# A decoder layer on one core: the opening put in the planner's order, and the conditioning of the output gates moved behind the attention

## The chip, the core and the metric

The kernel runs on one core of a Trainium2 chip. The number that counts is the device time of one execution in microseconds (us). The core has five engines with a queue each: TensorE (PE, matrix products into PSUM), VectorE (DVE), ScalarE (ACT), GpSimd (POOL) and SyncE (SP), which here issues nearly all DMAs. An engine takes its instructions strictly in the order of its queue, and one that has to wait holds everything behind it.

## The reference, cut to what matters

One layer of a decoder with a conditioning vector: 512 tokens of 1024 channels, fp32.

```python
cond = jax.nn.silu(c)                                        # 1024 numbers
ada = (cond @ ada_w[l] + ada_b[l])[:, None, :]               # 1024 x 6144
sh1, sc1, gt1, sh2, sc2, gt2 = jnp.split(ada, 6, axis=-1)    # 1024 each
h = modulate(rmsnorm(x, norm1_w[l]), sh1, sc1)               # h * (1 + sc1) + sh1
p = h @ w_in[l]                                              # all mixers' projections
...                                                          # A: HGRN2, B: sparse attention, C: RWKV7
merged = ga * (y_a @ w_branch[l, 0]) + gb * (y_b @ w_branch[l, 1]) + gc * (y_c @ w_branch[l, 2])
x = x + gt1 * (merged @ w_out[l])
h = modulate(rmsnorm(x, norm2_w[l]), sh2, sc2)
x = x + gt2 * ((jax.nn.silu(h @ ffn_w1[l]) * (h @ ffn_w3[l])) @ ffn_w2[l])
return rmsnorm(x, final_norm_w)
```

The product `cond @ ada_w` has 6144 columns, counted here in 12 blocks of 512: blocks 0 to 3 are sh1 and sc1, 4 and 5 gt1 (the gate on the output projection), 6 to 9 sh2 and sc2, 10 and 11 gt2 (the gate on the FFN).

## The kernel before, in words

**Products.** Every fp32 product is three fp32r products: a matrix is split into `hi` (a cast, on ACT for weights: `whi`, for activations: `hhi`) and `lo` (the difference, on DVE: `wlo`, `hlo`), and TensorE adds hi·hi, lo·hi and hi·lo in PSUM. A weight tile goes from a DMA (`wraw`, three buffers) over `whi` and `wlo` (two each) to `mm` (L438). `tr` (L442) and the transposes at L495 and L667 run on TensorE too. PSUM has four rings of two buffers, g, f, m and n. All other instructions are recorded at one helper line, L191, so they are told apart by their tiles.

**Stages, by the trace's time.** 0 to 66: the opening. Then phase A to about 510, in which the projections of the mixers A and C and of the attention are interleaved with these two mixers. The attention (`b_mixer`) with `merge(0)` and `merge(2)` to 693, `merge(1)` and the output projection to about 800, the FFN to the end.

**The opening.** `run` issues all its loads on SP: c, then the conditioning weights `aw` of the chunks k = 0 and 1 (128 rows of h each), the four x tiles, the identity, the small vectors `vrows` (norm weights, `ada_b` and the like, two tiles of rows that `turn_vecs` transposes into columns `vT`), then for each k the first input weights `fw` (768 columns) and `aw` of the next k. `FIRST` says for which k a conditioning load exists and how many chunks it covers: every k by itself. `norm_x` makes the RMS norm of x (a Square with accumulation on ACT, a power on POOL, then half the tile on DVE and half on ACT). `first_gemm` walks over k: `ada(k)` multiplies `aw` by `cond` and adds up on DVE (`ada_sum`, eight instructions into `facc`), adds over the partitions with products against `ones` on TensorE (`ada_cols`), which gives scale and shift; `modulate` transposes the chunk of x (4 transposes) and applies them (`nh` on ACT, then `hhi` and `hlo`); `products` makes the 18 products of this k into six PSUM tiles. Instructions are placed here by the framework's scheduler. `c_setup` then turns the six tiles into the first operands of mixer C.

**Phase A** is planned by `Order` with a `Clock`, which counts what each instruction costs and picks at each step among jobs (weight tiles, which feed TensorE) and chains (generators of mixer steps). It begins by `order.clock.reset()` after the opening. One of the chains, "D", is `ada_steps`: for each of the blocks 6, 7, 8, 9, 4, 5, 10, 11 it loads eight tiles `adaw` of 128x512 (two buffers, so that a load has to wait for the sum that read its buffer), adds them up on DVE into `adacc`, and adds over the partitions on TensorE. The gates' rows (4, 5, 10, 11) are written to a row `adarow` in DRAM, from which `gate_row` broadcasts them later.

**After phase A** the framework's scheduler places all instructions again. `merge(b)` multiplies each of the eight output tiles of branch b by its gate: for `merge(1)` each m needs a gate tile (24 products, from a `wraw` of `in_w_in`) and a branch tile (12 products, `in_w_branch`), and DVE does `msg` and the `wlo` of both.

## Time and profile before

| | |
|---|---|
| three timed runs | 1170.91, 1172.86, 1173.13 us, median 1172.86 |
| the profiled execution | 1168.5 us, span 1166.7, granted clock 0.993 |
| TensorE busy | 1113.3 us (95% of the span) |
| VectorE busy | 656.0 us (56%) |
| ScalarE busy | 415.4 us (36%) |
| DMA | 125.28 MB, mean 107 GB/s |

The span runs from the first to the last instruction; the execution's own time is 1.8 us longer. Busy matmuls overlap each other, so TensorE's pace is read from the starts of its instructions and its losses from its idle time.

### The profile page before, as it was taken

To read this page: it belongs to the slowest core of one execution; us is meant where nothing else is said; L and a number is where in the kernel's file an instruction comes from. 1 tells how busy PE (TensorE), PEld (TensorE's weight loads), DVE (VectorE), ACT (ScalarE), POOL (GpSimd) and SP (SyncE) were. 2 spreads that over 40 slices of the span, in tenths; PEclk is the share of its full clock that TensorE was granted. 3 is DMA by queue.
4 is the path that set the end of the run, shared out by engine and by line. 5 is a ranking of instruction groups with operands and counts; after the bars stand their busy time and mean duration, and the time that the engine had idled before them with its cause. 6 is when DMAs were issued, how large, how long until landed. Compare 5 with 4: busy or idle time off the path is not lost.

```text
span 1166.7 us, 18717 instructions
## 1 busy us (share of the span) xinstructions
PE 1113.3 (95%) x7545; PEld 908.2 (78%) x7545; DVE 656.0 (56%) x1404; ACT 415.4 (36%) x753; POOL 82.7 (7%) x96
## 2 busy tenths in 40 slices
PE   3989999999999999899999989999999999999997
PEld 3759887878887897577878667878888888888886
DVE  5858666675756766377576745445333433432533
ACT  4342431242331231165454654435222323222221
POOL 1001010120111000110112002110000000000000
PEclk9989999999999999999999999999999999999999
DMA  9934433324253234653223105542333333333331
GB/s 280 264 103 134 140 89 85 84 68 134 52 124 84 71 101 118 197 164 100 73 63 82 28 1 146 160 137 72 92 94 105 90 97 102 90 100 99 91 108 72
DMA packets 183087, 125.28 MB, mean 107 GB/s; under 512 B 27929, under 2 KB 163111, under 8 KB 183000
## 3 DMA queue, kind: packets, MB, share of 16 engines
q1 hardware_dynamic: 182424, 123.04, 37.2%
q8 instruction: 59, 0.97, 0.4%
q10 hardware_dynamic: 576, 1.05, 0.2%
q14 instruction: 28, 0.23, 0.1%
HBM read 121.15 MB, written 5.53 MB: 109 GB/s over the span
## 4 chain that ended last, share of the span: by engine, by line
PE 83%; DMA 5%; DVE 5%; SPq 2%; ACT 2%; issue 2%; POOL 0%; POOLq 0%; DVEq 0%; ACTq 0%
PE g L438 26%; PE f L438 25%; PE m L438 18%; PE n L438 11%; SPq L191 2%; PE n L442 2%; DMA adaw<-in_ada_w_dram 1%; DVE wlo L191 1%; DMA wraw<-in_w_in_dram 1%; DMA msg<-adarow 1%; PE m L442 1%; DMA x<-in_x_dram 1%; DMA fw<-in_w_in_dram 1%; ACT bpt L191 0%; DMA wraw<-in_w_out_dram 0%
## 5 line engine op out<-in xcount | busy, mean ns | idle before, releaser
L191 DVE TENSOR_TENSOR wlo<-wraw,whi 128x1024 fp32r<-128x1024 f32 (+2 forms) x144 | 164.2, 1140 | 154.9 <-ACT whi L191 153.0
L191 ACT CAST whi<-wraw 128x1024 fp32r<-128x1024 f32 (+2 forms) x144 | 139.1, 967 | 279.0 <-PE f L438 119.6
L438 PE MATMUL g<-hhi,whi 128*128 128x512 f32 (+1 forms) x368 | 154.7, 420 | 9.9 <-ACT whi L191 9.9
L438 PE MATMUL g<-hhi,wlo 128*128 128x512 f32 (+1 forms) x368 | 143.9, 391 | 2.5 <-DVE wlo L191 2.3
L438 PE MATMUL g<-hlo,whi 128*128 128x512 f32 (+1 forms) x368 | 143.3, 390 | 0.0
L438 PEld LDWEIGHTS g<-hhi,whi 128*128 128x128 f32 x368 | 70.1, 190 | 29.4 <-ACT whi L191 11.3
L438 PE MATMUL f<-hhi,whi 128*128 128x512 f32 (+1 forms) x240 | 92.7, 386 | 0.0
L438 PE MATMUL f<-hhi,wlo 128*128 128x512 f32 (+1 forms) x240 | 92.4, 385 | 0.0
L438 PE MATMUL f<-hlo,whi 128*128 128x512 f32 (+1 forms) x240 | 92.0, 383 | 0.0
L438 PEld LDWEIGHTS g<-hhi,wlo 128*128 128x128 f32 x368 | 69.7, 189 | 19.7 <-DVE wlo L191 4.9
L438 PEld LDWEIGHTS g<-hlo,whi 128*128 128x128 f32 x368 | 70.0, 190 | 11.2 <-issue 0.5
L191 DVE SCALAR_TENSOR_TENSOR adacc<-adaw,cond,adacc 128x512 f32<-128x512 f32 x56 | 42.6, 761 | 17.6 <-DMA adaw<-in_ada_w_dram 17.0
L438 PEld LDWEIGHTS f<-hhi,whi 128*128 128x128 f32 x240 | 45.4, 189 | 8.5
L438 PEld LDWEIGHTS f<-hhi,wlo 128*128 128x128 f32 x240 | 45.2, 188 | 8.6
L438 PEld LDWEIGHTS f<-hlo,whi 128*128 128x128 f32 x240 | 45.1, 188 | 8.2
L438 PE MATMUL f<-whi,hhi 128*128 128x256 f32 (+1 forms) x144 | 44.4, 308 | 0.0
L191 DVE CUSTOM_DVE_ANT_0 bs<-m,bW 128x128 f32<-128x128 f32 (+3 forms) x64 | 30.1, 486 | 24.5 <-PE m L438 15.3
L438 PE MATMUL f<-wlo,hhi 128*128 128x256 f32 (+1 forms) x144 | 41.6, 289 | 0.0
L438 PE MATMUL f<-whi,hlo 128*128 128x256 f32 (+1 forms) x144 | 41.5, 288 | 0.0
L191 ACT ACTIVATE bs<-bs,bst 128x128 f32<-128x128 f32 (+3 forms) x64 | 35.9, 563 | 12.8 <-DVE bst L191 12.4
L438 PE MATMUL f<-yhi,whi 128*128 128x512 f32 x96 | 38.3, 399 | 2.2 <-ACT yhi L191 1.4
L191 POOL TENSOR_TENSOR merged<-merged,msg 128x512 f32<-128x512 f32 x16 | 26.0, 1622 | 202.3 <-DVE msg L191 194.5
(439 smaller groups left out, 2375.9 us busy)
## 6 DMA issues: line engine op xcount, KB each, us to landing
wraw<-in_ffn_w_dram SPq DMA_DIRECT2D x66, 512.0 KB
wraw<-in_w_in_dram SPq DMA_DIRECT2D x52, 512.0 KB
adaw<-in_ada_w_dram SPq DMA_DIRECT2D x64, 256.0 KB
aw<-in_ada_w_dram SPq DMA_DIRECT2D x16, 512.0 KB
wraw<-in_w_branch_dram SPq DMA_DIRECT2D x16, 256.0 KB
wraw<-in_w_out_dram SPq DMA_DIRECT2D x8, 512.0 KB
fw<-in_w_in_dram SPq DMA_DIRECT2D x24, 128.0 KB
toep<-toep SPq DMA_DIRECT2D x8, 320.0 KB
```

Of the source, the lines that this page charges most:

```text
L191: r = f(*a, **kw)
L438: return self.nc.tensor.matmul(o, l, r, **kw)
L442: return self.nc.tensor.transpose(o, x, ident)
```

## The change

1. **Opening in the planner.** `norm_x`, `first_gemm`, `setup_vecs` and `c_setup` go; the opening is a set of chains and jobs of `Order`, written in the planned order, and phase A follows without a reset. x is loaded first. The vectors `vrows` are issued from POOL (12 DMAs, ahead of POOL's powers for the norm) instead of SP. Norms are whole-tile operations, two of the four sums of squares go to DVE (`tensor_tensor_reduce`). All 32 transposes of x are made ahead of the products, ACT copies them to SBUF (`xT`), and `first_mod` applies scale and shift from there. The first weight tile of mixer A (q, head 0) is split into buffers of its own during the opening.
2. **Conditioning of sh1 and sc1.** `FIRST = {0: 1, 1: 1, 2: 2, 4: 2, 6: 1, 7: 1}`: for k = 0 and 1 TensorE multiplies `aw` by `cond` directly, 16 products with one column each (`n<-cond,aw`), in place of DVE's sums; k = 2, 3 and k = 4, 5 are summed in pairs, 128x512 at a time. `aw` has three buffers of the double size in place of six, so the loads for k = 4, 6 and 7 wait for the sums or products of k = 0, 1 and 2.
3. **Gates.** Chain D does blocks 6 to 9 alone. Blocks 4 and 5 are issued in `merge(2)`, 10 and 11 in the FFN's tiles j = 4 and 9, each from a pool that is open there; the framework's scheduler places them.
4. **Planner.** Costs of DMAs, the rule when a job's tile is loaded or split, and `pace` (8 for 4) change; the bias of the attention gets a tile of its own.

The diff, cut (`Clock` and `Order` show the lines that set rates and pace):

```diff
-FIRST = {k: 1 for k in range(KT)}
+FIRST = {0: 1, 1: 1, 2: 2, 4: 2, 6: 1, 7: 1}
...
-            self.bus = max(self.bus, t + 1.3) + size / 3.3e5
-            return self.end(outs, ins, self.bus + 0.7)
+            took = size / (4.0e5 if run >= 4096 else 3.4e5 if run > 512 else 3.0e5)
...
-    def run(self, until=None, pace=4):
-        while until not in self.done and (self.chains or self.tiles or self.steps):
+    def run(self, until=lambda: False, pace=8):
+        while not until() and (self.chains or self.tiles or self.steps):
...
-            nc.sync.dma_start(rows[r0:r0 + n], ap)
+            nc.gpsimd.dma_start(rows[r0:r0 + n], ap)
...
-    def ada_steps(self):
-
-        nc, pool = self.nc, self.pc
-        self.ada_row = self.t(self.dr, [12, 512], "adarow")
-        blocks = (6, 7, 8, 9, 4, 5, 10, 11)
+    def ada_steps(self, pool, *blocks, acc="adacc"):
+
+        nc = self.nc
...
+    def first_ada(self, pool, ks):
...
+            if k < 2:
+
+                ps = None
+                for q in range(2):
+                    for a in range(2):
+                        yield self.cond, aw[:, a, 4 * q:4 * q + 4], ("now", "turned")[k], ":n" if ps is None else "now"
+                        if ps is None:
+                            ps = self.psn()
+                        for kk in range(4 * q, 4 * q + 4):
+                            self.mm(ps[:, a:a + 1], aw[:, a, kk], self.cond[:, kk:kk + 1], start=(kk + a == 0), stop=(kk + a == KT))
...
+            acc = self.t(pool, [P, 2, 2, P], "facc", bufs=2)[:, :, :n]
+            for kk in range(KT):
+                yield self.cond, aw[:, 0, kk], aw[:, 1, kk], "dve+"
+                self.ada_sum(acc, kk, aw[:, :, kk])
...
-            order.chain("D", self.ada_steps(), 5, None)
...
+            order.chain("D", self.ada_steps(self.pc, 6, 7, 8, 9), 5, None)
...
+            ada = self.ada_steps(wo, 4, 5, acc="wtmp")
             for _ in self.merge(2, yc, h):
+                for _ in range(5):
+                    next(ada, None)
+            for _ in ada:
                 pass
...
+                if j in (4, 9):
+                    for _ in self.ada_steps(p3, 10 + (j == 9)):
+                        pass
```

TensorE's queue from its first instruction on, before (`n` is a PSUM ring; `x` the four token tiles, `facc` the sums of the conditioning):

```order
L495 MATMUL n_201<-ident_97,vrows_9_99 128x56
L438 MATMUL n_212<-ones_175,facc_214 128x1 x2
L667 MATMUL n_213<-ident_97,x_89 128x128
L667 MATMUL n_213<-ident_97,x_91 128x128
L667 MATMUL n_213<-ident_97,x_93 128x128
L438 MATMUL n_212<-ones_175,facc_227 128x1 x2
L667 MATMUL n_213<-ident_97,x_95 128x128
L667 MATMUL n_213<-ident_97,x_89 128x128
L667 MATMUL n_213<-ident_97,x_91 128x128
L667 MATMUL n_213<-ident_97,x_93 128x128
L667 MATMUL n_213<-ident_97,x_95 128x128
L438 MATMUL m_206<-hhi_177,whi_269 128x512
```

And in the changed kernel, the same place:

```order
L452 MATMUL n_181<-ident_83,vrows_14_99 128x56
L448 MATMUL n_187<-cond_84,aw_126 128x1 x12
L452 MATMUL m_204<-ident_83,x_113 128x128
L452 MATMUL m_204<-ident_83,x_115 128x128
L452 MATMUL m_204<-ident_83,x_117 128x128
L452 MATMUL m_204<-ident_83,x_119 128x128
L452 MATMUL f_210<-ident_83,x_113 128x128
L452 MATMUL f_210<-ident_83,x_115 128x128
L452 MATMUL f_210<-ident_83,x_117 128x128
```

The transposes of one k stood before each k's products; now the conditioning products and the transposes of several k stand ahead of the first product (behind the rows shown come the rest of the eight groups of four transposes and four more products with `aw`, and then the first product of k = 0).

VectorE's queue at the end of the attention and the beginning of `merge(1)`, before (`ylo` is the last operation on the attention's output, `msg` the gating of an output tile, `wlo` a weight's split, `bkc` a part of `merged`):

```order
L191 TENSOR_SCALAR bs_6630<-bs_6630,bst_6631 128x512
L191 SCALAR_TENSOR_TENSOR ylo_7123<-y_5261,yhi_7122 128x4x128
L191 SCALAR_TENSOR_TENSOR msg_7132<-msg_7132,f_7205 128x512
L191 TENSOR_TENSOR wlo_7255<-wraw_7253,whi_7254 128x512
L191 TENSOR_TENSOR wlo_7280<-wraw_7277,whi_7279 128x1024
L191 SCALAR_TENSOR_TENSOR bkc_7607<-merged_4436,bq_7604 128x512
```

And in the changed kernel:

```order
L197 SCALAR_TENSOR_TENSOR ylo_7083<-y_5159,yhi_7082 128x4x128
L197 TENSOR_SCALAR wtmp_6663<-adaw_6659,cond_84 128x512
L197 SCALAR_TENSOR_TENSOR wtmp_6663<-adaw_6661,cond_84,wtmp_6663 128x512
L197 SCALAR_TENSOR_TENSOR wtmp_6663<-adaw_6665,cond_84,wtmp_6663 128x512
L197 SCALAR_TENSOR_TENSOR wtmp_6663<-adaw_6668,cond_84,wtmp_6663 128x512
L197 SCALAR_TENSOR_TENSOR wtmp_6663<-adaw_6725,cond_84,wtmp_6663 128x512
L197 SCALAR_TENSOR_TENSOR wtmp_6663<-adaw_6728,cond_84,wtmp_6663 128x512
L197 SCALAR_TENSOR_TENSOR msg_7092<-msg_7092,f_7165 128x512
L197 TENSOR_TENSOR wlo_7215<-wraw_7213,whi_7214 128x512
L197 SCALAR_TENSOR_TENSOR wtmp_6663<-adaw_6785,cond_84,wtmp_6663 128x512
L197 TENSOR_TENSOR wlo_7240<-wraw_7237,whi_7239 128x1024
L197 SCALAR_TENSOR_TENSOR wtmp_6663<-adaw_6788,cond_84,wtmp_6663 128x512
```

Six sums of block 4 (`wtmp`) now stand between `ylo` and the first `msg`, and two more before `bkc`; those of block 5 follow among the next tiles.

SyncE's queue at this place in the changed kernel (`adaw` are the tiles of block 4, `wraw` weight tiles: of a branch, of `w_out` and of a gate):

```order
L197 DMA wraw_7268<-in_w_branch_dram 64x4x128 x2
L197 DMA adaw_6659<-in_ada_w_dram 128x512
L197 DMA adaw_6661<-in_ada_w_dram 128x512
L197 DMA adaw_6665<-in_ada_w_dram 128x512
L197 DMA adaw_6668<-in_ada_w_dram 128x512
L197 DMA adaw_6725<-in_ada_w_dram 128x512
L197 DMA adaw_6728<-in_ada_w_dram 128x512
L197 DMA adaw_6785<-in_ada_w_dram 128x512
L197 DMA adaw_6788<-in_ada_w_dram 128x512
L197 DMA wraw_7290<-in_w_out_dram 128x1024
L197 DMA adaw_6791<-in_ada_w_dram 128x512
L197 DMA wraw_7296<-in_w_in_dram 128x8x128
```

Before, the loads of the branch tile, of `w_out` and of the gate followed each other here; now nine `adaw` loads stand among them, and from the third on each waits for the sum that read its buffer.

## Rows read from the trace of the kernel before

**Rows 1.** One execution by engine: busy us, share of the span, instructions

```profile
PE 1113.3 (95%) x7545; PEld 908.2 (78%) x7545; DVE 656.0 (56%) x1404; ACT 415.4 (36%) x753; POOL 82.7 (7%) x96
```

**Rows 2.** Page's costliest groups, chain D's sums: busy, mean ns | idle before

```profile
L191 DVE SCALAR_TENSOR_TENSOR adacc<-adaw,cond,adacc 128x512 f32<-128x512 f32 x56 | 42.6, 761 | 17.6 <-DMA adaw<-in_ada_w_dram 17.0
```

**Rows 3.** Windows: length; busy (instructions) of PE, PEld, DVE, ACT, POOL; PEclk; DMA; GB/s

```profile
0.00:20.00 20.00, 2.61 (x12) 2.45 (x12) 9.62 (x28) 8.65 (x15) 2.97 (x11) 1.00 0.91 268
72.00:76.00 4.00, 3.96 (x9) 2.22 (x8) 2.97 (x4) 0.47 (x1) 0.00 (x0) 0.50 0.50 143
460.00:480.00 20.00, 16.43 (x184) 10.80 (x184) 8.05 (x18) 2.86 (x4) 1.65 (x1) 1.00 0.53 147
480.00:500.00 20.00, 17.48 (x87) 11.46 (x86) 9.30 (x14) 4.88 (x7) 2.81 (x6) 1.00 0.78 235
```

**Rows 4.** Opening in order of time: start, length, engine, operation [idle before <-releaser]

```profile
12.71 1.06 ACT L191 ACTIVATE hhi<-x 128x1024 fp32r<-128x1024 f32 x1 [9.48 <-DMA x<-in_x_dram]
...
17.37 1.01 PE L438 MATMUL n<-ones,facc 128*128 128x1 f32 x4
...
20.40 0.82 ACT L191 CAST whi<-fw 128x768 fp32r<-128x768 f32 x1
20.42 0.96 DVE L191 TENSOR_TENSOR wlo<-fw,whi 128x768 fp32r<-128x768 f32 x1
21.12 0.77 ACT L191 ACTIVATE nh<-n,adaT,s 128x512 f32<-128x512 f32 x1
...
21.93 0.62 ACT L191 CAST hhi<-nh 128x512 fp32r<-128x512 f32 x1
...
21.95 1.12 PE L667 MATMUL n<-ident,x 128*128 128x128 f32 x4 [1.34 <-ACT nh L191]
...
22.72 1.20 PE L438 MATMUL m<-hhi,whi 128*128 128x512 f32 x2
```

**Rows 5.** TensorE after the opening, in order of time

```profile
71.57 0.79 PE L438 MATMUL g<-hhi,whi 128*128 128x512 f32 x1 [5.34 <-ACT whi L191]
```

**Rows 6.** Tile facc, all of its instructions: min/median/max ns, first and last start

```profile
L191 DVE SCALAR_TENSOR_TENSOR facc<-aw,cond,facc x56: 475/479/486, 8.4 to 54.9; 128x256 f32<-128x256 f32 x56
...
L438 PE MATMUL n<-ones,facc x32: 164/250/371, 17.4 to 56.8; 128*128 128x1 f32 x32
```

**Rows 7.** SyncE's issues in order of time, opening and end of phase A

```profile
10.03 0.32 SPq L191 DMA_DIRECT2D vrows<-in_ada_b_dram  x1
...
488.34 5.70 SPq L191 DMA_DIRECT2D adaw<-in_ada_w_dram  x2
494.15 1.00 SPq L191 DMA_DIRECT2D wraw<-in_w_in_dram  x2
```

**Rows 8.** The chain that ended last, by time: start, us, what

```profile
282.45 2.83 DMA adaw<-in_ada_w_dram
...
479.97 3.46 PE g L438 x15
...
487.87 6.60 DMA wraw<-in_w_in_dram
```

**Rows 9.** TensorE at the end of phase A, in order of time

```profile
476.38 0.50 PE L438 MATMUL g<-hhi,whi 128*128 128x512 f32 x1 [3.04 <-ACT whi L191]
```

**Rows 10.** VectorE at the beginning of merge(1), in order of time

```profile
693.49 0.69 DVE L191 SCALAR_TENSOR_TENSOR ylo<-y,yhi 128x512 fp32r<-128x512 f32 x1 [6.66 <-ACT yhi L191]
701.39 0.69 DVE L191 SCALAR_TENSOR_TENSOR msg<-msg,f 128x512 f32<-128x512 f32 x1 [7.22 <-PE f L438]
...
702.86 2.06 DVE L191 TENSOR_TENSOR wlo<-wraw,whi 128x1024 fp32r<-128x1024 f32 x1 [0.17 <-ACT whi L191]
...
723.52 1.22 DVE L191 TENSOR_TENSOR wlo<-wraw,whi 128x1024 fp32r<-128x1024 f32 x1
```

**Rows 11.** TensorE in merge(1), in order of time

```profile
702.23 0.47 PE L438 MATMUL f<-yhi,whi 128*128 128x512 f32 x1 [0.26 <-DVE msg L191]
```

**Rows 12.** VectorE in the FFN, in order of time

```profile
828.59 1.22 DVE L191 TENSOR_TENSOR wlo<-wraw,whi 128x1024 fp32r<-128x1024 f32 x1 [4.04 <-ACT whi L191]
```

More of the change, by code (lines that the diff above doesn't have):

```diff
@@ L243, in spend @@
         clock = self.clock
-        t = max([clock.at["PE"]] + [clock.ready(x) + 0.07 for x in (l, r)] +
-                [max(clock.read.get(x, 0.0), 0.0 if clock.by.get(x) else clock.wrote.get(x, 0.0)) + 0.07 for x in clock.keys(o)])
+        t = clock.start("PE", [o], [l, r], 1)
         if t > clock.at["PE"]:
@@ L262, in mark @@
     def mark(self, name, *aps):
-        self.done[name] = max([self.at] + [self.clock.ready(x) for x in aps])
+        self.done[name] = max(self.clock.ready(x) for x in aps)
     def advance(self, c):
@@ L292, in tend @@
     def tend(self):
-        loaded = sum(w.raw is not None and (w.w is None or w.split is None) for w in self.tiles)
+        loaded = sum(w.raw is not None and (w.w is None or w.split is None) for w in self.tiles if not w.early)
         loaded += bool(self.steps and self.tile.split is None)
@@ L297, in tend @@
             if w.raw is None:
-                if loaded >= 3:
+                if loaded >= 3 and not w.early:
                     break
                 w.prepare(self.clock, 0)
-                loaded += 1
+                loaded += not w.early
+            elif w.own and self.when(w.own) <= self.at:
+                w.prepare(self.clock, 1)
         for x, w in enumerate(self.tiles[:3]):
-            if all(n in self.done for n in w.needs):
+            if w.early or all(n in self.done for n in w.needs):
                 if x and self.tiles[0].hi is None:
@@ L307, in tend @@
                 break
-        if self.tiles and all(n in self.done for n in self.tiles[0].needs):
+        if self.tiles and (self.tiles[0].early or self.tiles[0].ahead or all(n in self.done for n in self.tiles[0].needs)):
             self.tiles[0].prepare(self.clock, 1)
@@ L355, with __init__ @@
 class Weights:
-    def __init__(self, load, split, steps, needs=(), ring="g"):
-        self.load, self.split, self.todo, self.needs, self.ring = load, split, steps, needs, ring
+    def __init__(self, load, split, steps, needs=(), ring="g", early=False, own=None, ahead=False):
+        self.load, self.split, self.todo, self.needs, self.ring, self.early, self.own, self.ahead = load, split, steps, needs, ring, early, own, ahead
         self.raw = self.w = self.hi = None
@@ L1131, in a_tile @@
         off = A_OFF + (0 if nm == "q" else 512) + 128 * hd
[L1132 removed]
+        return self.full(self.i["w_in"][0, :, off:off + 128], h, end, needs, dst)
     def a_mixer(self, y):
@@ L1608, in run @@
[L1608 to L1624 removed]
+            nc.scalar.activation(self.cond, self.cT, AF.Sigmoid)
@@ new lines, in run @@
+            V.tensor_tensor(self.cond, self.cond, self.cT, op=ALU.mult)
+            raw = self.bproj[2].rearrange("p a b -> p (a b)")[:, :MASKS.shape[1]]
+            order.done["now"] = 0.0
+            order.chain("load", self.first_loads(p0, raw), -1, None)
+            for j in range(4):
+                order.chain(f"nx{j}", self.first_norm(xs, j, p0), 1 + j / 10, None)
+            order.chain("tx", self.first_turn(xs), 2)
+            order.chain("vecs", self.turn_vecs(vrows[0]), 0, "n")
@@ L1634, in run @@
             order.job(*gt[:2], *[x for n in range(4) for x in (kt[2 * n], kt[2 * n + 1], gt[2 + n])], *gt[6:])
-            order.run("A")
+            order.run(lambda: f"h{KT - 1}" in order.done and not [w for w in order.tiles if w.early and w.w is None] and "vec1" in order.done)
+            ahead.close()
+            self.pc = pcs.enter_context(tc.tile_pool(name="pc", bufs=1))
+            with tc.using_default_side("right"):
+                self.pa = pas.enter_context(tc.tile_pool(name="pa", bufs=1))
+            yc, ya = self.new_y(), self.new_y()
+            order.chain("C", self.c_main(yc), 0)
+            order.chain("pre", self.c_pres(), 0.3)
+            order.chain("A", self.a_mixer(ya), 0.5, "n")
+            order.chain("D", self.ada_steps(self.pc, 6, 7, 8, 9), 5, None)
+            order.chain("bias", self.b_bias(self.bproj[2]), 6, None)
+            order.run(lambda: "A" in order.done)
             self.dump("ya", ya)
```

365 lines of the change are left out of this document (217 added, 148 removed).

## The prediction

> **What bounds the kernel now.** I read the busy times first: TensorE is busy for 1113.3 of 1166.7 us [rows 1], so a change pays only where TensorE stands or runs at its lower clock. The windows show where that is [rows 3]. In the first 20 us it works for 2.61, while the DMAs are busy at 0.91: the opening waits for its loads. At 72 to 76 the granted clock is 0.50, which is 1.2 GHz in place of 2.4. At 460 to 500 TensorE is idle for 20 - 16.43 + 20 - 17.48 = 6.1 us. Between these stretches it hardly waits. The rows of the opening in order of time come next [rows 4]: x is seen at 12.71, because the conditioning weights are loaded ahead of it; TensorE's first products against `ones` start at 17.37, and the first of the 144 products at 22.72. After them TensorE stands for 5.34 us, until 71.57, since the split of the first tile of mixer A comes behind the shifts of mixer C [rows 5]. It had lost its clock there: its first nine products take from 71.57 to about 76.1, 4.5 us in place of 9 x 0.23 = 2.1 (3.46 for 15 at full clock [rows 8]). So the opening costs as much as one that hands over at 74.0 with the clock up. Everything below is measured against these 74.0.
>
> **The opening, part by part.** *DVE's sums.* Before, 56 sums of 0.479 and 8 shorter ones [rows 6]. Now k = 0 and 1 need none and k = 2 to 5 take 16 wider ones of about 0.75 [rows 2]: DVE loses some 11 us of work, worth nothing in itself, since TensorE is the one that is late.
> *x first.* At 268 GB/s [rows 3], x (2.1 MB), the identity and the first half of `aw` for k = 0 (0.5 MB) need 9.9 us; with the start at 1.5 TensorE can begin the new products at about 11.4. The norm needs x at some 10, two halves of the sums side by side, the power and the scaling; by the lengths of [rows 4] it is done at about 14.5, ahead of its use.
> *TensorE up to the first product.* Four products against `ones` of 128x1 are two whole ones and take 1.01 cold [rows 4], so 0.5 each, and 0.25 warm (0.250 for an instruction, two to a product but overlapping, [rows 6]). Twelve with `aw`: 6.0, to 17.4. Then 24 transposes: 1.12 for four, cold [rows 4], gives 6.7 cold and, at the double clock, 3.4; with the clock rising on the way 4.4, to 21.8. Four more products 1.0, scale and shift 0.3, `nh` 0.77, `hhi` 0.62 [rows 4]: first product at **24.5**. If the clock rises as early as the first product of `aw` it is 22.5, if it doesn't rise at all before, 27.9. So the products start *later* than before (22.72).
> *From there on.* 144 products x 0.23 = 33.1; the 16 one-column products of k = 1 stand in the stream: 4.0; the second turn of vectors 0.3; twelve products against `ones` 3.0; no transposes any more, of which seven groups stood in the stream before. Waits: when k = 0 is through, `whi` 0.82 and `wlo` 0.96 of k = 2 [rows 4], four pair sums 3.0, `ones` 1.0, scale 0.3, `nh` 0.77, `hhi` 0.62 and seven hand-overs of 0.1 make 8.2, against 4.1 of k = 1's products and the 1.0 counted already: 3.1 exposed. For k = 4 and k = 7, which have more cover, I take half of it each: 3.0. Sum 24.5 + 33.1 + 4.0 + 0.3 + 3.0 + 6.1 = **71.0**. The tile of mixer A is split by then (its buffers are its own), so there is neither gap nor loss of clock: 71.0 against 74.0, **-3.0**. Ends: 22.5 and half the waits give 66, 27.9 and waits of 8 give 76.3: -8 to +2.
>
> **Phase A without four blocks of chain D.** 32 loads and 32 sums (24 us of DVE) leave. No wait of TensorE hangs on the sums themselves, so they are worth 0. The loads are another thing at the end of phase A: SP's issue of two `adaw` at 488.34 holds the queue for 5.70, the second waits for a sum, and two `wraw` loads come out only behind it at 494.15 [rows 7]; the chain that ended last goes through a `wraw` that landed after 6.60 us [rows 8], and one wait on `whi` took 3.04 [rows 9]. I give back all 2.5 of 480 to 500 and 1.5 of the 3.6 of 460 to 480: **-4** (0, if other loads take the place, to -6). All of phase A is planned anew with other rates; the products are the same, and I count it 0 with 3 to either side.
>
> **Blocks 4 and 5 in merge(1).** All 16 sums stand there in DVE's queue. DVE has room (7.22 idle before `msg` at 701.39 [rows 10]), but the loads don't come in a stream: two buffers, so two loads, two sums, two loads. A load takes 2.83 [rows 8], a sum 0.76 [rows 2], so a pair costs about 3.8, and six sums behind `ylo` (693.49 + 0.69) with the first pair there already end at about 694.2 + 1.5 + 2 x 3.7 = 703.1 in place of 701.39. Behind them wait `msg` and the `wlo` of the branch tile, for which TensorE waits at 702.23 [rows 11]: +1.7. The seventh sum, again one load later (at about 706.5), stands ahead of the gate's `wlo`, which began at 702.86 [rows 10]: that tile is ready about 0.6 later still, **+2.3** in all. The ladder of block 5 starts when block 4's row is stored, at about 714, and its seventh sum ends after four loads at some 729; the gate's `wlo` behind it, at 723.52 before [rows 10], ends at about 730.5 where 728.5 would do: **+1.9**. SP's queue is held as well: `w_out` and gate tiles stand behind `adaw` loads that wait for sums, which is in these sums. Together **+4.2**; at best the loads come early and it is 1, at worst each of the eight pairs of loads shows with half its length, 11.
>
> **Blocks 10 and 11 in the FFN.** DVE stands for 4.04 before a `wlo` [rows 12], more than the two or three sums that fall into such a gap; 0, or +2 if a `wlo` comes late. The four one-row products are moved only.
>
> **Sum.** -3.0 - 4 + 4.2 = -2.8. The profiled 1168.5 (1166.7 and 1.8 around it) becomes 1165.7; the median of the runs, 1172.86, lies 4.4 above that execution, and the same difference gives **1170.1**.
>
> **The rivals.** *A, better: 1164.* The clock comes up with the first one-column products, the planner's opening runs as it counts (hand-over at 68), and the ladder hides in DVE's 7.22: -6 - 4 + 1 = -9. For it: TensorE has work from 11 us on; against: the two-buffer ladder shows in chain D already, where DVE stood 17.0 us for `adaw` [rows 2].
> *B, cancels: 1173.* The end of phase A keeps its waits, since 3.04 of them belong to a split behind a load that no `adaw` delays: -3 + 4.2 - 1.
> *C, slower by the ladder: 1177.* Each load of blocks 4 and 5 is exposed on SP's queue too, where the gate tiles wait: +8 to +9 there, -3 in the opening, little at the end of phase A. It decides from about 8 us of waits in merge(1).
> *D, slower by POOL: 1177.* POOL issues 12 loads before its first power. SP needs 0.32 for such an issue [rows 7]; with that POOL is free at 5. No POOL issue is in the trace. Up to 1.0 each (free at 13) the norm of x is hardly later; beyond that every 0.1 costs 1.2, so at 1.5 each +6, and the opening turns from -3 to +3 or more. I take the near row, so 0.
> On this, the Trainium skill, page "DMA: Bandwidth & Descriptors", section "Latency and other measured facts", gives about 1 us for the first byte of a load issued from GpSimd, and "SBUF — State Buffer", section "SBUF: two separate sides", says that a VectorE operation in a two-port mode keeps GpSimd from writing the descriptors meanwhile; by these the issues would end at or past the point where D begins. No run here shows it so far.
>
> **How the numbers follow.** A measurement here can tell about 0.2%, 2.3 us, from no change. Chances: forecast 0.42 (1167 to 1173; three quarters of it beyond 0.2%), A 0.17, B 0.19, C 0.12, D 0.10. Faster 0.31 + 0.17 = 0.48; within 0.2%: 0.11 + 0.17 of B = 0.28; slower 0.12 + 0.10 + 0.02 = 0.24. The range reaches from A's near side to C and D: 1163 to 1177.
>
> **What would show it.** First product at 24 to 25 and the first tile of mixer A at about 71 with a clock of 1.00 (right), or a first power on POOL later than 13 (D). In 460 to 500 less than 3 us of TensorE idle. In merge(1) waits of TensorE on `msg` or `wlo` of 4 us in all, with DVE waiting for `adaw`; 1 or less is A, 8 or more C. In the FFN none. It is wrong if phase A as a whole takes a different length: I can't see that from the old trace.

## The result and the profile after

The changed kernel takes 1178.11 us (median of 5 runs, 1176.43 to 1180.41), the kernel before 1171.35 beside it (5 runs, 1170.54 to 1173.13): a ratio of 1.007, 95% interval 1.0043 to 1.0097. It is slower, by 0.7%. The forecast was 1170.1, and its range ended at 1177. The profiled execution took 1176.74 us, span 1175.0, granted clock 0.99; against the profile of before (1168.5) that is +8.2 where -2.8 was forecast.

TensorE, by the page's first row, is now busy for 15.1 us more than in [rows 1], with nearly as many products. By the table further down 12.8 of these lie in the opening (85.3 - 16.8 = 68.5 busy, 82.3 - 26.6 = 55.7 before), where TensorE now starts early, on narrow products and at the lower clock.

```profile
PE 1128.4 (96%) x7601; PEld 920.6 (78%) x7601; DVE 649.3 (55%) x1372; ACT 420.2 (36%) x758; POOL 90.5 (8%) x108
```

**The opening**, in order of time (start, length, engine, operation, idle before and its releaser):

```profile
1.32 0.75 POOL L197 DMA_DIRECT2D vrows<-in_norm_w_dram  x1 [0.44 <-issue]
...
4.16 0.52 POOL L197 DMA_DIRECT2D vrows<-in_rw_a_dram  x1
...
5.47 1.06 ACT L197 ACTIVATE hhi<-x 128x1024 fp32r<-128x1024 f32 x1 [2.23 <-DMA x<-in_x_dram]
...
9.52 3.23 POOL L197 TENSOR_TENSOR rs<-rs,mhalf 128x1 f32<-128x1 f32 x4
...
10.64 5.25 PE L448 MATMUL n<-cond,aw 128*128 128x1 f32 x24 [0.18 <-DMA aw<-in_ada_w_dram]
...
15.75 1.09 PE L452 MATMUL m<-ident,x 128*128 128x128 f32 x4
...
23.81 1.28 PE L448 MATMUL g<-hhi,whi 128*128 128x512 f32 x2 [1.07 <-ACT hhi L197]
```

x is used at 5.47 in place of 12.71 [rows 4]. POOL issues at 0.52 each and reaches its first power at 9.52. The first product stands at 23.81 (24.5 forecast). But it runs at the lower clock, and that is where the opening is lost. (The trace has no record of the clock before 20.8 and shows 1.00 there; the 24 one-column products at 10.64 take 5.25, where at the higher clock e4 below has 2.81.) TensorE further on, and below it the windows (length, busy of PE, PEld, DVE, ACT, POOL, granted clock, DMA share, GB/s):

```profile
27.45 3.71 PE L448 MATMUL n<-cond,aw 128*128 128x1 f32 x32
...
33.24 1.05 PE L448 MATMUL g<-hlo,whi 128*128 128x512 f32 x2
...
36.99 0.62 PE L448 MATMUL m<-hhi,wlo 128*128 128x512 f32 x2
...
40.38 0.58 PE L448 MATMUL n<-ones,facc 128*128 128x1 f32 x4 [0.96 <-DVE facc L197]
...
43.76 0.73 PE L448 MATMUL g<-hhi,whi 128*128 128x512 f32 x2 [1.95 <-ACT hhi L197]
...
45.73 1.05 PE L448 MATMUL g<-hhi,wlo 128*128 128x512 f32 x2
```

```profile
24.00:28.00 4.00, 4.00 (x13) 3.03 (x13) 1.92 (x4) 2.92 (x6) 0.00 (x0) 0.57 1.10 380
28.00:32.00 4.00, 4.00 (x32) 3.79 (x32) 1.31 (x6) 0.41 (x1) 0.00 (x0) 0.88 1.10 376
32.00:36.00 4.00, 4.00 (x14) 3.21 (x13) 1.91 (x3) 1.64 (x3) 0.00 (x0) 0.69 0.99 287
...
40.00:44.00 4.00, 1.42 (x9) 1.28 (x10) 2.83 (x8) 1.73 (x3) 0.00 (x0) 1.00 0.65 186
44.00:48.00 4.00, 4.00 (x12) 3.08 (x12) 3.85 (x6) 1.78 (x3) 0.00 (x0) 0.59 0.99 325
...
460.00:480.00 20.00, 15.59 (x73) 10.22 (x72) 3.15 (x4) 1.64 (x2) 2.81 (x6) 0.91 0.46 133
480.00:500.00 20.00, 18.76 (x107) 12.99 (x105) 5.62 (x10) 6.97 (x11) 0.00 (x0) 1.00 0.53 145
```

Two wide products take 1.05 at 33.24 and 0.62 at 36.99: 1.2 and 2.4 GHz. The low stretches stand behind three things: the transposes and the wait in front of the first product; the one-column products of k = 1 at 27.45, during which TensorE did not stand at all; and 40 to 44, in which it was busy for 1.42 of 4. In 40 to 44 the window shows 1.00, and the two products at 43.76 still take 0.73; at 45.73 it is 1.05, so here the fall comes with the work after the pause.

**The end of phase A.** The windows 460 to 500 hold 4.4 + 1.2 = 5.6 us of idle TensorE (6.1 before [rows 3]). TensorE there, SyncE's queue, and the chain that ended last:

```profile
474.78 0.80 PE L448 MATMUL g<-hhi,whi 128*128 128x512 f32 x1 [3.14 <-ACT whi L197]
```

```profile
485.38 7.40 SPq L197 DMA_DIRECT2D wraw<-in_w_in_dram  x3
```

```profile
467.99 5.68 DMA wraw<-in_w_in_dram
...
485.38 6.10 DMA wraw<-in_w_in_dram
```

The wait on `whi` is 3.14 (3.04 in [rows 9]), the queue is held for 7.40 where [rows 7] showed 5.70, and no `adaw` stands near. In the kernel before, the chain that ended last shows where its 3.04 came from:

```profile
470.52 4.74 DMA wraw<-in_w_in_dram
475.29 1.05 ACT whi L191
```

This `wraw` was issued at 470.52, with no `adaw` holding the queue ahead of it, and the wait at 476.38 ended 12 us before the hold of 488.34 in [rows 7] began.

**merge(1)**, VectorE and then TensorE, against [rows 10, 11]:

```profile
696.67 1.54 DVE L197 SCALAR_TENSOR_TENSOR wtmp<-adaw,cond,wtmp 128x512 f32<-128x512 f32 x2 [2.16 <-DMA adaw<-in_ada_w_dram]
700.32 1.54 DVE L197 SCALAR_TENSOR_TENSOR wtmp<-adaw,cond,wtmp 128x512 f32<-128x512 f32 x2 [2.11 <-DMA adaw<-in_ada_w_dram]
701.78 0.68 DVE L197 SCALAR_TENSOR_TENSOR msg<-msg,f 128x512 f32<-128x512 f32 x1
```

```profile
702.61 0.47 PE L448 MATMUL f<-yhi,whi 128*128 128x512 f32 x1 [1.50 <-DVE msg L197]
726.77 0.50 PE L448 MATMUL g<-wolo,bq 128*128 128x512 f32 x1 [0.23 <-DVE wolo L197]
730.36 0.50 PE L448 MATMUL f<-hhi,wlo 128*128 128x512 f32 x1 [1.92 <-DVE wlo L197]
```

The ladder shows as drawn: two loads, two sums at once, the next two loads. TensorE waits 1.50 + 0.23 + 1.92 = 3.65 (0.26 before [rows 11]), and after the last of these it works at the lower clock for 3.4 us, which costs 1.7 more:

```profile
732.00:734.00 2.00, 2.00 (x6) 1.60 (x5) 1.66 (x2) 0.63 (x1) 0.64 (x1) 0.50 0.59 162
```

**By stage.** For every run I summed windows of 2 us between events of the profiled execution: ScalarE's first read of mixer A's first tile (`aq<-g`), the last `ylo`, and the first use of the output projection's result with its gate (`wtmp<-f,msg`). The last column runs from the last `hlo` of the second norm to the FFN's last column tile (`glo`); the rest of the output projection, 41.3 before and 39.7 changed, lies between and is not in the table. Each cell is the length / the idle time of TensorE in it / the loss to the clock (length times one minus the granted clock), in us.

| kernel | opening | phase A and attention | merge(1) | FFN, first part |
|---|---|---|---|---|
| before | 82.3 / 26.6 / 3.4 | 611.2 / 17.6 / 3.4 | 72.9 / 0.3 / 0 | 234.1 |
| changed | 85.3 / 16.8 / 5.1 | 607.3 / 17.8 / 3.4 | 80.5 / 3.7 / 1.7 | 237.0 |
| e1 gates back in A | 83.8 / 17.3 / 5.1 | 619.6 / 22.5 / 6.8 | 72.3 / 0.3 / 0 | 234.1 |
| e2 gates moved only | 82.0 / 25.5 / 1.7 | 612.6 / 16.3 / 10.2 | 81.0 / 3.7 / 1.7 | 236.4 |
| e3 sums on DVE | 87.6 / 28.0 / 10.2 | 606.8 / 14.6 / 6.8 | 80.7 / 4.0 / 1.7 | 237.7 |
| e4 wide first | 81.8 / 10.4 / 6.8 | 611.0 / 18.6 / 6.8 | 81.8 / 5.3 / 1.7 | 236.6 |
| e5 interleaved | 86.2 / 15.8 / 6.9 | 613.5 / 19.7 / 8.5 | 80.5 / 3.8 / 1.7 | 236.8 |
| e6 pace 4 | 85.6 / 16.8 / 5.1 | 617.1 / 22.5 / 8.5 | 81.4 / 4.1 / 1.7 | 237.2 |
| e7 blocks 4, 5 in A | 85.1 / 16.9 / 5.1 | 621.1 / 21.9 / 12.0 | 72.6 / 0.3 / 0 | 237.0 |
| e8 e4 + e5 + e7 | 81.2 / 9.5 / 6.8 | 610.1 / 16.5 / 5.1 | 74.2 / 1.8 / 0 | 236.5 |
| e9 old rules | 84.3 / 16.9 / 5.1 | 620.1 / 20.4 / 15.4 | 81.4 / 4.3 / 1.7 | 237.0 |
| e10 waits filled | 82.3 / 8.4 / 6.8 | 612.5 / 17.3 / 6.8 | 72.3 / 0.3 / 0 | 237.0 |
| e11 no chain D | 83.6 / 16.8 / 5.1 | 609.4 / 19.1 / 6.8 | 80.8 / 4.1 / 1.7 | 236.7 |
| e12 and a fourth buffer | 86.4 / 16.9 / 6.8 | 607.2 / 17.9 / 6.8 | 80.7 / 4.1 / 1.7 | 236.9 |

The loss to the clock in phase A differs from kernel to kernel (3.4 to 15.4), mostly with no edit that goes with it, and the granted clock of one kernel differs between its executions (0.980 to 0.993 over 20 of the kernel before), so phase A is compared without it below: 611.2 - 3.4 = 607.8 before, 603.9 changed. The rows of e4, e5 and e7 are of executions 4.1, 4.1 and 6.6 above their medians.

With the new opening ScalarE takes that first tile up late: at 85.3 in the changed kernel, 2.7 behind the start of the tile's last product (0.2 in the kernel before). So about 2 us in the opening's cell of such a row are time in which TensorE already works on phase A. Against `before` and e2, its phase A is about 2 longer than its cell says.

### The profile page after: what moved, and what is told of

It reads as the page before. It is cut to its first block, busy times and chain, and to the rows that moved or that the text cites. A ratio compares the mean times of both kernels' runs of the same rounds, so it can differ in the third digit from the quotient of the medians.

```text
span 1175.0 us, 18832 instructions
## 1 busy us (share of the span) xinstructions
PE 1128.4 (96%) x7601; PEld 920.6 (78%) x7601; DVE 649.3 (55%) x1372; ACT 420.2 (36%) x758; POOL 90.5 (8%) x108
## 3 DMA queue, kind: packets, MB, share of 16 engines
q10 hardware_dynamic: 576, 1.05, 0.2%
## 4 chain that ended last, share of the span: by engine, by line
PE 80%; DMA 7%; DVE 6%; ACT 3%; SPq 2%; issue 2%; POOL 1%; POOLq 0%; DVEq 0%; ACTq 0%
PE g L448 26%; PE f L448 22%; PE m L448 18%; PE n L448 11%; SPq L197 2%; PE n L452 2%; DMA adaw<-in_ada_w_dram 2%; DMA aw<-in_ada_w_dram 1%; DMA wraw<-in_w_out_dram 1%; DVE wlo L197 1%; DMA wraw<-in_w_in_dram 1%; PE m L452 1%; DMA msg<-adarow 1%; DVE wtmp L197 1%; ACT whi L197 1%
## 5 line engine op out<-in xcount | busy, mean ns | idle before, releaser
L197 DVE TENSOR_TENSOR wlo<-wraw,whi 128x1024 fp32r<-128x1024 f32 (+2 forms) x143 | 161.6, 1130 | 157.4 <-ACT whi L197 156.9
L448 PE MATMUL g<-hhi,whi 128*128 128x512 f32 (+1 forms) x360 | 151.3, 423 | 8.4 <-ACT hhi L197 4.8
L448 PE MATMUL g<-hhi,wlo 128*128 128x512 f32 (+1 forms) x360 | 140.8, 395 | 1.8 <-DVE wlo L197 1.8
L448 PE MATMUL g<-hlo,whi 128*128 128x512 f32 (+1 forms) x360 | 139.6, 391 | 0.0
L197 DVE SCALAR_TENSOR_TENSOR adacc<-adaw,cond,adacc 128x512 f32<-128x512 f32 x42 | 31.4, 748 | 20.5 <-DMA adaw<-in_ada_w_dram 20.2
L197 ACT ACTIVATE bs<-bs,bst 128x128 f32<-128x128 f32 (+3 forms) x64 | 35.7, 560 | 18.6 <-DVE bst L197 18.3
```

What stands on the lines that cost most here:

```text
L197: r = f(*a, **kw)
L448: return self.nc.tensor.matmul(o, l, r, **kw)
```

## The experiments

**e1: the gates back in chain D.** Everything else of the change stays.

```diff
-            order.chain("D", self.ada_steps(self.pc, 6, 7, 8, 9), 5, None)
+            order.chain("D", self.ada_steps(self.pc, 6, 7, 8, 9, 4, 5, 10, 11), 5, None)
...
-            ada = self.ada_steps(wo, 4, 5, acc="wtmp")
...
-                if j in (4, 9):
```

> The changed kernel with the gates' blocks 4, 5, 10 and 11 back in chain D of phase A (nothing of them in the merges or the FFN). Theory 1, the ladder costs what it shows: from the end of the attention on the changed kernel lost 6.2 us in merge(1) and the output projection and 2.8 in the FFN, 9.0 in all; 4.1 of it are the four one-row products themselves, which go back into phase A, and 4.9 are waits, which go: 1178.1 - 4.9 = 1173, with no wait of TensorE on msg or on a gate tile's wlo above 0.5 in merge(1). Theory 2, the loads of chain D hold the end of phase A, and the change did gain there: phase A gets longer by 4 beyond the products: 1177, with idle time of TensorE in the last 60 us of phase A at 12 in place of 8.5.

Measured: 1178.92, ratio 1.0063 (1.0042 to 1.0085), no better than the changed kernel. The ladder is gone (merge(1) 72.3, FFN 234.1), but phase A took the gain back: 612.8 without the clock's loss, 8.9 more than with the gates out. Of that, 4.1 are the gates' own one-row products and 4.7 are waits, most of them at the end of phase A, as theory 2 had it. One wait on `whi` is longer than in either kernel, and the chain that ended last leads to it through an `adaw`, which held the queue until 475.06:

```profile
482.29 0.79 PE L448 MATMUL g<-hhi,whi 128*128 128x512 f32 x1 [4.80 <-ACT whi L197]
```

```profile
470.92 2.93 DMA adaw<-in_ada_w_dram
...
474.73 0.34 SPq L197
...
475.16 6.00 DMA wraw<-in_w_in_dram
```

So in the new plan the gates' loads did hold the end of phase A. But the new plan with all blocks is 612.8 - 607.8 = 5.0 us longer in phase A than the old plan (about 7 with the 2 us that its opening's cell holds), and 4.9 of its waits are new (22.5 for 17.6).

**e2: only the gates moved.** The kernel before, with part 3 of the change alone.

```diff
-            order.chain("D", self.ada_steps(), 5, None)
+            order.chain("D", self.ada_steps(self.pc, 6, 7, 8, 9), 5, None)
...
+            ada = self.ada_steps(wo, 4, 5, acc="wtmp")
...
+                if j in (4, 9):
+                    for _ in self.ada_steps(p3, 10 + (j == 9)):
```

> The kernel before with only the gates' blocks moved: chain D does blocks 6 to 9, blocks 4 and 5 in merge(2), 10 and 11 in the FFN; opening and planner as before. Theory 1: phase A is shorter by the four one-row products (4.1) and keeps its waits of about 7.5 at its end; merge(1) and FFN lose the 9.0 seen in the changed kernel: 1171.4 + 4.9 = 1176. Theory 2, phase A's end was held by these loads: it is shorter by another 4: 1172, with 3.5 of idle time between 455 and 520 in place of 7.5.

Measured: 1178.12, ratio 1.0059 (1.0039 to 1.008). Moving the gates costs, by itself, about as much as the whole change. merge(1) is 8.1 longer; phase A lost 5.4 without the clock's part, of which 4.1 left with the products and only 1.3 are waits. At the end of phase A it won more, 2.6 of idle TensorE in 460 to 500 where the kernel before has 6.1, and the wait of 3.04 is not there; but 2.1 of idle time in 410 to 450, where there was none, took most of that back. With 5.2 in 455 to 520 the measurement lies between the two theories there.

```profile
410.00:450.00 40.00, 37.86 (x455) 32.93 (x454) 20.72 (x42) 12.77 (x32) 4.08 (x4) 0.91 0.29 76
460.00:480.00 20.00, 19.18 (x154) 13.99 (x149) 5.66 (x9) 4.16 (x6) 5.37 (x7) 0.91 0.39 114
480.00:500.00 20.00, 18.24 (x100) 12.43 (x98) 5.62 (x10) 6.54 (x11) 0.00 (x0) 1.00 0.69 190
```

```profile
485.56 0.50 PE L438 MATMUL g<-hhi,whi 128*128 128x512 f32 x1 [0.80 <-ACT whi L191]
```

**e3: the conditioning of k = 0 and 1 on VectorE again**, in the new opening.

```diff
-            if k < 2:
+            if k < 0:
```

> The changed kernel with the conditioning of k = 0 and 1 summed on VectorE again (eight instructions of 128x256 each) and added up by products against ones, so that the two blocks of 16 one-column products with aw go; all else as changed. Theory 1, these products leave TensorE at its lower clock: the sums of k = 0 end by about 17, soon after their last load, the first product comes at 21 to 22 in place of 23.8, the block of 16 between 27 and 31 goes, and with it the fall of the clock at 31 to 34: the first tile of mixer A starts at 70 to 72 in place of 75.2, time 1173 to 1175. Theory 2, the clock falls because of the waits for DVE alone: DVE gets 7.6 us more work ahead of k = 2's sums, which wait as long as this, and the tile starts at 75 to 79: 1178 to 1182.

Measured: 1175.92, ratio 1.0041 (1.0015 to 1.0066). The first product comes at 21.20, earlier, but TensorE then waits for the sums, and the opening ends at 87.6:

```profile
31.08 0.99 PE L448 MATMUL n<-ones,facc 128*128 128x1 f32 x4 [4.78 <-DVE facc L197]
...
39.70 1.01 PE L448 MATMUL n<-ones,facc 128*128 128x1 f32 x4 [6.37 <-DVE facc L197]
```

```profile
32.00:36.00 4.00, 1.08 (x5) 0.93 (x4) 2.65 (x7) 0.00 (x0) 0.00 (x0) 0.50 1.07 319
```

The clock is low here from 29 to 50, without any one-column product with `aw`: it falls within the first of these two waits, as theory 2 had it. Within the new opening the one-column products are the better choice, then. The total is 2.2 below that of the changed kernel, but the intervals of the two ratios overlap; what is lower lies in phase A (600.0 without the clock's loss), and why, I can't explain.

**e4: eighteen unused wide products first**, on zeros, while TensorE has nothing to do.

```diff
+            wd = self.t(p0, [P, T], "nh", bufs=2)
+            wr = h[1][:, 1]
+            V.memset(wd, 0.0)
+            nc.scalar.copy(wr, wd)
+            pw = self.psum("f")
+            for _ in range(18):
+                self.mm(pw, wr[:, :P], wr, start=True, stop=True)
```

> The changed kernel with 18 more products of 128x512 on zeros at its very beginning, ahead of x's arrival, while TensorE has nothing to do (some 3 to 11 us); their result is not used. Theory 1, the clock rises with such products and one-column products and transposes do not hold it: granted clock 1.0 by about 9, transposes between 16 and 21 at the low clock's 1.06 for four again, first products cold as in the changed kernel, time within 1 us of 1178. Theory 2, any work of TensorE holds the clock once it is up: the transposes take 0.6 for four, the first product comes at about 21, none of k = 0's products is slow, 1174 or less.

Measured: 1173.62, ratio 1.0022 (1.0003 to 1.004), 4.5 below the changed kernel.

```profile
2.70 6.58 PE L448 MATMUL f<-hlo 128*128 128x512 f32 x18 [2.70 <-ACT hlo L197]
...
10.83 2.81 PE L448 MATMUL n<-cond,aw 128*128 128x1 f32 x24
13.50 1.01 PE L452 MATMUL m<-ident,x 128*128 128x128 f32 x4
...
21.08 0.98 PE L448 MATMUL g<-hhi,whi 128*128 128x512 f32 x2 [1.07 <-ACT hhi L197]
...
30.02 1.05 PE L448 MATMUL f<-hlo,whi 128*128 128x512 f32 x2
```

The 24 one-column products take 2.81 in place of 5.25, the first product comes 2.7 earlier, and the opening is 3.5 shorter. So up to there it was the clock. But neither theory holds whole: the transposes at 13.50 still take 1.01 for four, the first products are slow as before, and the low stretches behind the one-column products and behind the pause at 36 to 39.5 stay. (The table's 6.8 can't be set against the changed kernel's 5.1: here the clock is on record from 7.4 on, there from 20.8.)

**e5: the one-column products of k = 1 between the wide ones.**

```diff
-                        yield self.cond, aw[:, a, 4 * q:4 * q + 4], ("now", "turned")[k], ":n" if ps is None else "now"
+                        yield self.cond, aw[:, a, 4 * q:4 * q + 4], ("now", f"j{3 + 2 * q + a}")[k], ("now", "turned")[k], ":n" if ps is None else "now"
```

(`j3` to `j6` are marked by pairs of products of k = 0.)

> The changed kernel with the 16 one-column products of k = 1 no longer in one block: they stand in four groups of four between the pairs of 128x512 products of k = 0. Theory 1, a stretch of one-column products alone makes the clock fall behind it: the granted clock stays at 1.0 between 28 and 36 (in the changed kernel one stretch of 3.4 us at 0.5 there, worth 1.7), and the first tile of mixer A ends about 1.5 earlier than 85.3; 1176 to 1177. Theory 2, the clock falls because TensorE had stood shortly before: the stretch stays somewhere between 24 and 36, nothing is gained, 1178.

Measured: 1180.14, ratio 1.0077 (1.0052 to 1.0103). The stretch at the lower clock stays, as theory 2 had it, and falls on more work (6.9 us lost for 5.1), so the one-column products' standing in one block is not what begins it:

```profile
24.00:28.00 4.00, 3.94 (x11) 3.00 (x11) 1.09 (x2) 3.17 (x7) 0.00 (x0) 0.58 0.89 269
...
32.00:36.00 4.00, 4.00 (x14) 3.33 (x14) 2.01 (x5) 1.02 (x2) 0.00 (x0) 0.50 0.74 241
```

**e6: `pace` 4 for 8** in all of the changed kernel.

```diff
-    def run(self, until=lambda: False, pace=8):
+    def run(self, until=lambda: False, pace=4):
```

> The changed kernel with the planner's pace of 4 again in place of 8; all else as changed. Theory 1, the new plan of phase A is worse because of the pace (with all blocks in chain D its phase A is 5 us longer than before without the clock's stretches): idle time of TensorE from 85 to the end of the attention falls from 17.8 to 14 or less, 1174. Theory 2, the pace doesn't matter, and the waits on wraw at the end of phase A come from the loads' own order: 17 to 19, within 1 of 1178.

Measured: 1190.94, ratio 1.0164 (1.0115 to 1.0213). The new pace is no cause of the loss; the new plan needs it: with 4, phase A has 4.7 us more of waits and loses 5.1 more to the clock.

**e7: blocks 4 and 5 back in chain D**, 10 and 11 left in the FFN.

```diff
-            order.chain("D", self.ada_steps(self.pc, 6, 7, 8, 9), 5, None)
+            order.chain("D", self.ada_steps(self.pc, 6, 7, 8, 9, 4, 5), 5, None)
...
-            ada = self.ada_steps(wo, 4, 5, acc="wtmp")
```

> The changed kernel with blocks 4 and 5 back in chain D of phase A, 10 and 11 still in the FFN. Theory 1, the ladder in merge(1) is the whole loss there: merge(1) to the output projection's first rows takes 72.5 us in place of 80.5, phase A gets the two products (2.0) and half of the waits that four blocks brought (half of 4.7): 1178.1 - 8.0 + 4.4 = 1174.5. Theory 2, the waits come back in phase A whatever the number of blocks: + 2.0 + 4.7 and one more stretch at the low clock, 1177 to 1179.

Measured: 1176.81, ratio 1.0045 (1.002 to 1.007). merge(1) is 72.6 again; phase A pays with 21.9 of waits and a wait of 3.96 on `whi` at 486.49.

**e8: e4, e5 and e7 together** (their edits as shown).

> Three of these together: blocks 4 and 5 in chain D, the one-column products of k = 1 in four groups, and the 18 unused products of 128x512 on zeros at the very beginning. If the losses add up (3.5 of the opening's clock and its earlier first product, 1.5 for the groups, 3.5 for the ladder): 1170, that is 0 to 3 below the kernel before. If phase A takes back what the opening gains: 1173 to 1175.

Measured: 1171.86, ratio 1.0009 (0.9983 to 1.0035): the loss is gone, and nothing is won.

**e9: the planner's old rules after the opening.**

```diff
+            if self.old:
+                self.bus = max(self.bus, t + 1.3) + size / 3.3e5
+                return self.end(outs, ins, self.bus + 0.7)
...
-            order.run(lambda: "A" in order.done)
+            order.run(lambda: "A" in order.done, 4)
```

> The changed kernel, with the planner's old rules from the end of the opening on: the old rate of the DMAs, the old rule for a tile's load and split, pace 4. Measured without the loss of clock, phase A and the attention took 607.8 us before and 603.9 changed, though four one-row products of 4.1 us in all have left them; with all blocks of the conditioning kept there in the new plan it was 612.8. Theory 1: the new rules make the worse plan. Then this stage takes 600 or less here (its waits 14 or less in place of 17.8), and the time is about 1173. Rival: the rules don't matter, the tiles come late because three buffers of wraw are too few at that place: 603 or more, with a wait of TensorE on whi or wlo behind a late load of wraw at 460 to 500, and a time of 1177 or more.

Measured: 1190.02, ratio 1.0162 (1.0124 to 1.0201). This edit holds the pace of 4 as well, which alone gave 1190.94 (e6); so beside it the old rules change nothing that can be told from noise, and with the pace of 8 they were not run. Phase A's waits are 20.4, with one of 2.10 behind a `wraw` at 493.93, as the rival had it.

**e10: e4 and e7 with TensorE's other two pauses in the opening filled.**

```diff
+    def hold(self, ps, n):
+        w = self.h[1][:, 7]
+        for _ in range(n):
+            self.mm(ps[:, P:], w[:, :P], w[:, P:], start=True, stop=True)
...
+            self.hold(ps, {2: 9, 4: 4}.get(k, 0))
```

> Gates of blocks 4 and 5 back in phase A, 18 unused products of 128x512 ahead of the conditioning products (as in the run with the wide products first), and unused products of 128x384 in the opening's two other waits of TensorE (nine behind the conditioning of k = 2, 3, four behind that of k = 4, 5). Nothing is left out of the computation. Theory 1: the opening loses its clock because TensorE stands or works narrow there. Then no stretch at a granted clock of 0.5 begins between 36 and 60 us, the opening's loss of clock falls from 6.8 to 3.5 or less, and mixer A's first tile ends at 79 to 80 in place of 81.8: the time is about 1170 to 1173. Rival: the fillers only delay the products behind them, or the clock falls at the one-column and transposing stretches whatever stands between them: the loss stays at 6.8 and the opening is as long or longer, with 1176 as in the run with the output gate in phase A.

Measured: 1172.59, ratio 1.0015 (0.9998 to 1.0032). The loss to the clock stays at 6.8, as the rival said: the low stretch now falls on the fillers (nine of 128x384 in 3.14), is shorter behind them, and comes again after the second pause. The time lies in theory 1's range all the same, by what e10 shares with e8 (1171.86).

```profile
37.38 3.14 PE L448 MATMUL n<-hlo 128*128 128x384 f32 x9 [0.25 <-DVE adaT L197]
...
42.44 0.62 PE L448 MATMUL m<-hhi,wlo 128*128 128x512 f32 x2
...
52.96 1.22 PE L448 MATMUL g<-hhi,whi 128*128 128x512 f32 x2
```

**e11: no chain D at all**, sh2 and sc2 left out. **e12: the same, with a fourth buffer** for weight tiles in phase A.

```diff
-            order.chain("D", self.ada_steps(self.pc, 6, 7, 8, 9), 5, None)
...
-                if loaded >= 3 and not w.early:
+                if loaded >= 4 and not w.early:
...
+        if pc is not None and self.nw % 4 == 0:
+            raw = self.t(pc, [P, 1024], "wrax", bufs=1)
```

> The changed kernel without chain D: the conditioning blocks 6 to 9 (sh2 and sc2) are left out, zeros stand for them. So phase A has no load adaw and no sum adacc at all; merge(2) and the FFN keep theirs. Sixteen one-column products and 32 sums are gone with it. Theory 1: the waits at the end of phase A stand behind adaw loads. Then phase A and the attention have 13 us of TensorE idle or less in place of 17.8, and the time is about 1173. Rival: the splits there wait for wraw loads that come out only when one of the three buffers is free, whatever adaw does: idle stays at 16 to 19, a wait on whi or wraw of 2 us or more stands between 460 and 500, and the time is 1176 to 1178.

> The same, sh2 and sc2 left out, and in phase A every fourth weight tile is loaded into a buffer of its own (wrax), so that four tiles can be on their way in place of three. Theory: the three buffers hold the loads back at the end of phase A. Then the idle time of phase A and the attention falls by 4 us or more against the run with three buffers and no chain D, and so does the time. Rival: the loads are late for another reason (they are planned late, or the DMAs are slow there): less than 1.5 us of difference.

Measured: 1177.34, ratio 1.0068 (1.0041 to 1.0095), and 1176.96, ratio 1.0065 (1.0044 to 1.0086). With no `adaw` load in phase A the waits of e11 are 19.1, and none of these is the conditioning's. TensorE waits

```profile
469.22 0.43 PE L448 MATMUL f<-wraw,msg 128*62 128x256 f32 x1 [1.14 <-DMA wraw<-in_nsa_cmp_w_v_dram]
472.05 0.50 PE L448 MATMUL g<-hhi,whi 128*128 128x512 f32 x1 [1.75 <-ACT whi L197]
...
511.42 0.80 PE L448 MATMUL g<-hhi,wlo 128*128 128x512 f32 x1 [2.17 <-DVE wlo L197]
```

The fourth buffer takes 1.2 off the waits, and the time stays; the pause at 472 turns into one for a step of the mixer:

```profile
473.10 0.63 PE L452 MATMUL m<-ident,X 128*128 128x128 f32 x4 [1.53 <-DVE X L197]
```

So the theory that three buffers hold the loads back falls as a cause of more than about one microsecond.

## Why the prediction was wrong, point by point

Profile against profile, the time went from 1168.5 to 1176.74.

**The opening, -3.0 forecast, +1.2 measured; this step failed.** Mixer A's first tile runs at full clock and ends such that its first products, at full pace, would stand at 75.2, against the 74.0 that the opening before was worth. All terms up to the first product held (23.81 for 24.5), the tile was split in time, and the waits were near what I took (0.96 and 1.95 around k = 2, 0.91 and 0.89 later). What failed is "neither gap nor loss of clock": 5.1 us went to the clock between 24 and 48. 71.0 - 0.7 + 5.1 = 75.4. The 1.2 is one execution's: the same opening in e1, e6, e7, e9 and e11 puts that product at 73.5 to 75.5, with 5.1 lost in each. I had costed the rise of the clock ahead of the first product and never its fall after the narrow products and the pauses that I had listed myself. e4 shows the part that can be had: 3.5 us of the opening. One bound of the range was wrong too: with the clock up from the first of these products on, the forecast's own terms give 11.4 + 3.0 + 3.4 + 1.0 + 1.7 = 20.5 for the first product and not 22.5; e4 has 21.08.

**Phase A, -4 forecast, with 0 for the new plan; the second of these failed, and it is the largest miss.** Phase A and the attention are 3.9 shorter without the clock's loss by the table, 2.0 from TensorE's side, and 4.1 us of one-row products left the stage (I had called them moved, with no price, since a sum over the whole kernel doesn't see them). So the stage lost about 2 where 4 were to be won. Its waits in four kernels tell the two parts of the change apart: 17.6 before, 16.3 with the gates moved out of the old plan (e2), 22.5 with them kept in the new plan (e1), 17.8 changed. The gates' leaving took off 4.7 in the new plan, about what was forecast, and 1.3 in the old one. What failed is "All of phase A is planned anew ... I count it 0 with 3 to either side": the new plan with the same blocks adds 4.9 of waits and 5.0 of length, about 7 from TensorE's side. The pace is not the cause of that (e6); what is, the runs don't show.

My reading of the rows was wrong as well. I had taken the queue held by `adaw` at 488.34 [rows 7] as the cause of the wait of 3.04 [rows 9], which stands at 476.38, ahead of it, and of the late `wraw` of [rows 8], which was issued at 487.87, ahead of it too (with no `adaw` near, the load at 485.38 still takes 6.10). The condition of rival B, that the end of phase A keeps its waits because the split there hangs on a load that no `adaw` delays, was right for the changed kernel (5.6 for 6.1, and a wait of 3.14); its time of 1173 did not come.

**The ladder in merge(1), +4.2 forecast: right.** 3.65 of waits, 3.4 more than before, where and how it was drawn (`msg` at 701.78, then a `wlo`). merge(1) and `w_out` together are 5.9 longer: 2.0 of moved products, 1.7 of clock behind the longest wait, some 2.3 of net waits, since `w_out` itself waits less. I had not costed the clock there. The lower clock in merge(1) goes with the ladder: 1.7 in each of the nine kernels that have it, 0 in the five that don't. Rival C, with 8 us of waits, did not come; that the time ended near its 1177 is chance. Rival A fell with both of its conditions: the hand-over came at 75.2 and not at 68, and the ladder did not hide.

**The FFN, 0 forecast: right as to the waits** (0.2); it is 2.9 longer, 2.0 by the moved products, the rest is open.

**Rival D fell.** POOL's issues cost 0.75, 0.56 and then 0.52 each, and the power began at 9.52, before the point of 13 that I had set. The Trainium skill, page "DMA: Bandwidth & Descriptors", section "Latency and other measured facts", gives about 1 us for the first byte of such a load; no run here tells that figure apart from the loads' own times, and the issuing engine was held for 0.52.

**The sum by steps:** 1.2 in the opening, -2.0 in phase A and the attention, 5.9 in merge(1) and `w_out`, 2.9 in the FFN and 0.3 behind it are 8.3. With the one-row products counted where they stood before, the miss of some 11 us is 4.2 in the opening, 6.1 in phase A, -0.3 in merge(1) and `w_out`, 0.9 in the FFN and 0.3 behind it.

**What stays open.** The two halves of the change don't add up: the gates alone cost 0.59% (e2), opening and planner alone 0.63% (e1), both 0.70%. The plan is made anew for each list of chains, and phase A comes out between 600.0 and 612.8 without its clock's loss. The waits at its end have several causes at once (a load, a split, a step of the mixers), and taking one away brought the next. Nor is it settled how much of the loss is the clock's. The profiled execution of the kernel before is among its best (0.993); over all executions on record the mean granted clock is 0.988 for both kernels (66 of the one, 0.980 to 0.993; 5 of the other, 0.986 to 0.990), by span times one minus clock some 14 us for either. The changed kernel's stretches in the opening and in merge(1) come back in every trace that has these pieces, so the kernel before must lose more elsewhere on average; where, its one trace doesn't show. More buffers for `adaw` in merge(1), and the blocks 4 and 5 in the attention's pool, were not tried.

## What to carry to other kernels

A queue that is held by one load beside a late one is not yet its cause: ask which of the two was issued first, and whether the late load could have started earlier at all with the other gone. A plan that is made anew has a price of its own, here 5 us or more with the same work: measure the new plan with the old work before the work is moved. When work moves onto TensorE in narrow pieces, or the pieces leave pauses, price the products behind them at the lower clock, 1.7 us for each such stretch of 3.4 us here. And side work that is moved out of a planned stretch into a scheduled one must bring its buffers along: two buffers turned a stream of loads into a ladder of 3.7 us for two (696.67 and 700.32), and whatever stood behind it in VectorE's queue climbed with it.

## What the hardware showed that was not expected

Stretches at 1.2 GHz of 3.4 us, worth 1.7 each, stood in the changed kernel's opening (6.8 us in e4, 20.5 in e3), one of them also after a stretch in which TensorE was busy all the time, but with one-column products (27.45 to 31.1, then 1.05 for two wide products where 0.62 is usual). Filling a pause with wide products moved the stretch onto the fillers and did not remove it (e10). Whether narrow products or pauses begin such a stretch these runs don't separate: in e3 one begins within a wait, and the changed kernel one behind narrow products without a pause. The same opening fell to 1.2 GHz at 24.2 and 31.0 in the changed kernel and at 29.4 in e11, so the places of the stretches are not fixed by the instructions alone. The Trainium skill, page "TensorE: Matmul & The Clock Gate", section "HAM oscillation — how this bites in real kernels", tells of a clock that falls when TensorE waits between groups of products; the stretch behind 44, after two waits of 0.96 and 1.95, agrees with it, and the one behind 31, with TensorE busy for all of 28 to 32, shows that no wait just before is needed. What began the stretches in phase A, of which each kernel has others, the runs don't show.
